# First MLP: gates and ups by seven block products for eight, plain downs woven between them, block sums from the attention's last head pair on

## The chip, the cores and the metric

The kernel runs on one core of one Trainium2 chip. Its five engines work from queues of their own and meet at semaphores: TensorE (PE in the profile; PEld is its weight load), VectorE (DVE), ScalarE (ACT), GpSimd (POOL) and SyncE (SP), which issues the loads. GpSimd issues a second kind of transfer, one that adds to what stands in memory. The metric is the device time of one execution in microseconds; less is better.

## The reference

A decoder trunk of two layers on 528 tokens (16 learned ones ahead of 512) with 1024 features: forgetting attention, a gated MLP, a gated linear recurrence (HGRN2), and a second gated MLP. All in float32. The part that the change touches is the MLP, here the first:

```python
def conv_ffn(h, norm_g, w_gate, w_up, conv_w, conv_b, w_down):
    xn = rms_norm(h, norm_g)
    a = xn @ w_gate                      # 1024 -> 2816
    ...
    a = (conv_b + conv_w[0] * a_pad[:, 0:L] + conv_w[1] * a_pad[:, 1:L + 1]
         + conv_w[2] * a_pad[:, 2:L + 2])    # causal, over the tokens
    return (jax.nn.silu(a) * (xn @ w_up)) @ w_down     # 2816 -> 1024
```

## The kernel before, in words

*Numbers.* Features lie on the partitions and tokens on the free axis. Every float32 operand of a matmul is split in two parts, hi and lo, and a product is three matmuls: hi by hi, hi by lo, lo by hi (`proj_unit`). `weights` loads one block of weights from HBM (SP, tile `raw`), copies it to `hi` (ScalarE, L210) and subtracts to get `lo` (VectorE, L126). The residual `h` stays in SBUF.

*Seven products for eight.* A product of 2 x 2 blocks is made from seven block products by Strassen's scheme in Winograd's form. It needs sums of weight blocks and sums of input blocks. The weights' sums are made ahead in HBM by DMA alone (`sum_blocks`): SP copies one block (L230) and GpSimd issues accumulating transfers on top (L232). For one key that is four copies and five accumulations, in four steps; accumulations onto the same sum, and the fourth sum, which takes in the second, wait for those before them. A generator, `summing`, holds all keys in order, and each call of `weights` (with `step` set) moves it one step on. The transfers go to SP's and GpSimd's queues, in order with what else stands there.

*Stages.* `fox` (attention) works on head pairs in a hand-written weave of generators; in its last turn, p = 7, `stage_p` makes early parts of the output projection, and after the turns the projection follows, with `summing` set ahead of it. `ffn0` is the first MLP, `hgrn` the recurrence, `ffn1` the second MLP.

*The first MLP (`ffn0`).* It has two runs of hidden features (`RUNS`: 2 x 6 and 2 x 5 blocks of 128). In each, `hidden` makes gate and up of one block with plain products (2 weights x 8 blocks x 3 matmuls x two halves of 264 tokens), the convolution, the gate; `forms` builds the seven input forms; then `down` multiplies by the down weights in seven block products for four pairs of output blocks. Sums are made of the down weights: 8 keys of 6 or 5 blocks' width. `hidden` has its memset of the first two columns of `A` on GpSimd (L1106).

*The second MLP (`ffn1`).* Its hidden pairs are split in five runs (`PAIRS`: 1, 2, 3, 2, 3 pairs of two blocks). The first pair (`plain`) uses plain products while the input forms are made. Every other pair uses `seven` twice, for its gates and its ups: seven products of 4 blocks x 3 matmuls, from the input forms and from a key's sums of gate or up weights. The downs (`down`) are plain products, woven between the next run's sevens:

```python
weave((chain(*steps), cost), side or (None, 1.0))
side = down(j0, hidden, i == len(runs) - 1), 5.3 * r
```

`weights` has four raw and four split buffers there (`self.more`), two and three elsewhere. Instructions are put in order per engine when the program is built, from the written order and a model of their times.

Of the kernel before, what the change touches and what calls it, by code (L numbers as in the profile page):

```python
# [12 lines left out]
F32 = mybir.dt.float32  # L13
# [8 lines left out]
P = 128  # L22
D = 1024
# [6 lines left out]
RUNS = [(0, 6), (12, 5)]  # L30
# [52 lines left out]
class Builder:  # L83
# [44 lines left out]
    def setup(self):  # L128
# [32 lines left out]
        self.summing = iter(())  # L161
        self.sqp = self.pool("sqp", 2)
# [19 lines left out]
    def weights(self, src, n, w=P, parts=1, step=True):  # L182
# [19 lines left out]
        if parts == 1:  # L202
            if isinstance(src, tuple):
                nc.sync.dma_start(raw[:, : n * w // 2], src[0])
                self.load = nc.sync.dma_start(raw[:, n * w // 2 :], src[1])
            else:
                self.load = nc.sync.dma_start(raw, src)
            if step:
                next(self.summing, None)
            nc.scalar.copy(hi, raw)  # L210
            self.sub(lo, raw, hi.bitcast(F32))
            return u
# [3 lines left out]
    def sum_blocks(self, key, blocks, joined=False):  # L216
# [7 lines left out]
        sums = [new(i, n) for i in range(2 if joined else 4)]  # L224
        if joined:
            both = new(2, 2 * n)
            sums += [both[:, :n], both[:, n:], both]
        s1, s2, s3, s4 = sums[:4]
        for out, x, *rest in (s1, w21, w22), (s2, w21, w22, w11), (s3, w11, w21), (s4, w12, s2):
# [3 lines left out]
            if out is s4:  # L233
                self.sums[key] = sums
            yield 1

    def down_blocks(self, mp, c0, r):

        w = self.a["dn0"]
        return [w[2 * mp + m][:, (c0 + k * r) * P : (c0 + k * r + r) * P] for m in range(2) for k in range(2)]  # L240

    def hidden_blocks(self, j, i):

        w = self.a["gu1"]
        return [w[2 * j + m, i][:, 4 * k * P : 4 * k * P + 4 * P] for m in range(2) for k in range(2)]

    def all_sums(self):
        for c0, r in RUNS:
            for mp in range(KT // 2):
                yield from self.sum_blocks((0, mp, c0), self.down_blocks(mp, c0, r))  # L250
        for j in range(PAIRS[0], NF // 2):
            for i in range(2):
                yield from self.sum_blocks((1, j, i), self.hidden_blocks(j, i), True)
# [127 lines left out]
    def fox(self, ctx):  # L381
# [285 lines left out]
        for p in range(-3, NPAIR):  # L667
            fill, cost = [], 0.0
# [33 lines left out]
        self.summing = self.all_sums()  # L702
# [117 lines left out]
    def hgrn(self, ctx):  # L820
# [237 lines left out]

        plan = {5: (0, 1, 2), 6: (3, 4, 5), 7: (6, 7)}
# [21 lines left out]
    def ffn0(self, ctx):  # L1081
        nc, a = self.nc, self.a
        layer, a0, o0 = 0, 0, 0
        ga, up = (halves(t0) if T - t0 > 512 else [(t0, T - t0)] for t0 in (a0, o0))
        gcol, cw, cb = ((V_FFN0, V_CW0, V_CB0), (V_FFN1, V_CW1, V_CB1))[layer]
        sp = self.pool(f"ffn1_{layer}", 1, ctx=ctx)
        s2 = self.pool(f"ffn2_{layer}", 2, ctx=ctx)
        self.normsplit(gcol, a0)
        segs = (SEG0, SEG1)[layer]
        am, rs = self.token_stats(segs)  # L1090
        self.spread_rs(rs, segs)
        def unit(w, toks, x):
            for t0, tn in toks:
                ps = self.anybank()[:, :tn]
                for _ in self.proj_unit(ps, w, x, t0, tn):
                    pass
                yield ps, t0, tn

        n = T - o0
        hw = n // 2  # L1100

        def hidden(m, early=None):

            A, t, s = (temp(w, nm) for w, nm in ((T + 2, "A"), (n, "t"), (n, "s")))
            if o0 == 0:
                nc.gpsimd.memset(A[:, 0:2], 0.0)  # L1106
            wg, wu = (self.weights(a[f"gu{layer}"][m, i], KT) for i in range(2))
            if early is not None:
                early()
            for ps, t0, tn in unit([wg], ga, self.x):  # L1110
                nc.vector.tensor_tensor(A[:, 2 + t0 : 2 + t0 + tn], ps, self.rsb[:, t0 : t0 + tn], ALU.mult)
            c0 = cw + 3 * m
            nc.scalar.activation(
                t, A[:, o0 + 2 : T + 2], AF.Identity, scale=self.vcol(c0 + 2), bias=self.vcol(cb + m)
            )
            nc.vector.scalar_tensor_tensor(t, A[:, o0 + 1 : T + 1], self.vcol(c0 + 1), t, ALU.mult, ALU.add)
            nc.vector.scalar_tensor_tensor(t, A[:, o0:T], self.vcol(c0), t, ALU.mult, ALU.add)
            self.act(s, t, AF.Silu)
            nc.vector.tensor_tensor(t, s, self.rsb[:, o0:], ALU.mult)
            for ps, t0, tn in unit([wu], up, self.x):  # L1120
                tv = t[:, t0 - o0 : t0 - o0 + tn]
                nc.vector.tensor_tensor(tv, ps, tv, ALU.mult)
            return t

        def temp(w, name):
            return s2.tile([P, 6 * P], F32, name=name, tag="temp", bufs=8)[:, :w]

        def put_form(f, j, x, fhi, flo):
            x = x.rearrange("p (f t) -> p f t", t=hw)
            f = slice(f, f + x.shape[1])  # L1130
            nc.scalar.copy(fhi[:, f, j, :], x)
            self.sub(flo[:, f, j, :], x, fhi[:, f, j, :].bitcast(F32))

        def forms(j, c0, r, fhi, flo, early):

            form = lambda f, x: put_form(f, j, x, fhi, flo)
            t1 = hidden(c0 + j)
            x11, x12 = t1[:, :hw], t1[:, hw:]
            ta, tb = temp(n, "ta"), temp(n, "tb")
            self.sub(ta[:, :hw], x11, x12)  # L1140
            form(0, x11)
            form(3, ta[:, :hw])
            t2 = hidden(c0 + r + j, early)
            x21, x22 = t2[:, :hw], t2[:, hw:]
            nc.vector.scalar_tensor_tensor(ta[:, hw:], ta[:, :hw], -1.0, x22, ALU.mult, ALU.subtract)
            form(4, ta[:, hw:])
            form(1, t2)
            self.sub(tb[:, :hw], x22, x12)
            nc.vector.scalar_tensor_tensor(tb[:, hw:], ta[:, hw:], -1.0, x21, ALU.mult, ALU.subtract)
            form(5, tb)  # L1150

        def parts(raw):

            w = raw.shape[1]
            hi = self.whi.tile([P, 8 * P], F32R, name="hi", tag="hi")[:, :w]
            lo = self.wlo.tile([P, 8 * P], F32R, name="lo", tag="lo")[:, :w]
            nc.scalar.copy(hi, raw)  # L1157
            self.sub(lo, raw, hi.bitcast(F32))
            return hi, lo

        def left(mp, c0, r, i):


            raw = temp(r * P, "left")
            if isinstance(i, int):
                src = self.sums[layer, mp, c0][i - 1]
            else:
                k0 = (c0 + i[1] * r) * P
                src = a[f"dn{layer}"][2 * mp + i[0]][:, k0 : k0 + r * P]
            nc.sync.dma_start(raw, src)  # L1170
            return parts(raw)

        def down(mp, c0, r, fhi, flo, last, first):

            def product(ps, w, f, start):
                hi, lo = w
                mm = nc.tensor.matmul  # L1180
                for k in range(r):
                    c = slice(k * P, k * P + P)
                    xh, xl = fhi[:, f, k, :], flo[:, f, k, :]
                    mm(ps, hi[:, c], xh, start=start and k == 0, stop=False, skip_group_check=not start)  # L1184
                    mm(ps, hi[:, c], xl, start=False, stop=False, skip_group_check=not start)  # L1185
                    mm(ps, lo[:, c], xh, start=False, stop=k == r - 1, skip_group_check=not start)  # L1186

            def put(m, half, ps, op, store=False):
                c = o0 + half * hw
                hv = self.h[:, 2 * mp + m, c : c + hw]  # L1190
                nc.vector.tensor_tensor(hv, hv, ps, op)
                if store and last and layer == 1:
                    nc.sync.dma_start(a["out"][2 * mp + m][:, half * hw : half * hw + hw], hv)

            A, D = (self.bank("p")[:, :hw] for _ in range(2))
            B, C = (self.bank(x)[:, :hw] for x in "cd")
            ws = lambda i: left(mp, c0, r, i)
            product(A, first[0] if first else ws((0, 0)), 0, True)
            nc.scalar.copy(B, A)
            product(D, first[1] if first else ws(1), 3, True)  # L1200
            put(1, 1, D, ALU.subtract)
            product(B, ws(2), 4, False)
            nc.scalar.copy(C, B)
            put(0, 1, B, ALU.add)
# [8 lines left out]
            if last and layer == 0:  # L1213
                self.sumsq(2 * mp)
                self.sumsq(2 * mp + 1)
# [317 lines left out]
```

## Time and profile before

| what | value |
|---|---|
| time, median of 3 runs (lowest to highest) | 1459.96 us (1459.2 to 1460.03) |
| the profiled execution's own time | 1463.9 us |
| its span | 1462.0 us |
| TensorE, share of the span | 98% |
| VectorE, ScalarE, GpSimd | 67%, 45%, 10% |
| mean granted TensorE clock | 0.994 |
| moved by DMA | 230.97 MB, mean 158 GB/s |
| first MLP, first to last matmul | 390.9 to 763.6 us |
| recurrence | about 764 to 1103 us |
| second MLP | about 1103 to 1462 us |

Durations and windows below are in microseconds from the span's start. The DMA share of a window is the mean busy share of the core's 16 DMA engines; q1 is the queue of SP's transfers, q0 that of GpSimd's. A matmul's record is longer than the distance to the next, since matmuls overlap, so the pace is read from counts or from starts.

### The profile page before, as it was taken

The numbers are of one execution on the slowest core, as the hardware profiler recorded it, in microseconds if no ns is written. First come the engines' busy times: TensorE is split into PE (matmuls) and PEld (weight loads), VectorE is DVE, ScalarE is ACT, GpSimd is POOL, SyncE is SP. The second block draws the span as 40 slices with busy tenths as digits, with TensorE's granted clock in tenths as the row PEclk, the third lists the DMA queues.
The fourth block names the chain that finished last, engine by engine and source line by source line (L and its number), as shares of the span: only waits on it lengthen the run. The fifth ranks groups of instructions, "written<-read, shape, count | busy, mean of one in ns | idle before, by whom it ended". The sixth has DMA issues, their size and how long they took to land.

```text
span 1462.0 us, 29172 instructions
## 1 busy us (share of the span) xinstructions
PE 1435.2 (98%) x11482; PEld 1349.0 (92%) x11482; DVE 974.9 (67%) x2079; ACT 663.1 (45%) x1293; POOL 150.2 (10%) x265
## 2 busy tenths in 40 slices
PE   7999999999999999999999999999999999999998
PEld 6888888888999999999999999999999889999997
DVE  6555555774667675666785667587567777866773
ACT  5355555563434444333563224333345565544551
POOL 6000000001112100112001101011111110000000
PEclk9999999999999999999999999999999999999999
DMA  4433334435999884678737617374587795544542
GB/s 160 119 105 90 90 90 123 124 99 137 293 231 247 213 254 137 171 193 197 218 92 181 168 22 181 91 178 103 126 238 169 208 265 162 173 143 137 161 146 85
DMA packets 99696, 230.97 MB, mean 158 GB/s; under 512 B 13528, under 2 KB 15320, under 8 KB 99560
## 3 DMA queue, kind: packets, MB, share of 16 engines
q1 hardware_dynamic: 79400, 188.47, 40.3%
q0 software_dynamic: 20160, 40.64, 18.3%
q8 instruction: 90, 1.47, 0.4%
q14 instruction: 46, 0.38, 0.1%
HBM read 213.62 MB, written 75.24 MB: 198 GB/s over the span
## 4 chain that ended last, share of the span: by engine, by line
PE 91%; DMA 4%; DVE 2%; ACT 1%; issue 1%; SPq 1%; ACTq 0%; DVEq 0%
PE psp L263 9%; PE psp L267 9%; PE psp L266 9%; PE pss L263 8%; PE pss L267 8%; PE pss L266 8%; PE psp L312 5%; PE psc L797 2%; PE psp L1292 2%; PE psp L1290 2%; PE psp L1291 2%; PE psp L1184 1%; PE psp L1186 1%; PE psp L1185 1%; PE pss L951 1%; PE psd L1292 1%
## 5 line engine op out<-in xcount | busy, mean ns | idle before, releaser
L210 ACT CAST hi<-raw 128x1024 fp32r<-128x1024 f32 (+3 forms) x250 | 234.1, 939 | 381.3 <-PE psp L266 96.1
L126 DVE TENSOR_TENSOR lo<-raw,hi 128x1024 fp32r<-128x1024 f32 (+3 forms) x254 | 275.5, 1088 | 100.9 <-ACT hi L210 96.8
L263 PE MATMUL psp<-xhi,hi 128*128 128x264 f32 (+1 forms) x984 | 283.9, 290 | 6.1 <-ACT xhi L332 6.1
L266 PE MATMUL psp<-xlo,hi 128*128 128x264 f32 (+1 forms) x984 | 283.6, 288 | 3.2 <-DVE xlo L333 3.2
L267 PE MATMUL psp<-xhi,lo 128*128 128x264 f32 (+1 forms) x984 | 283.9, 289 | 0.0
L263 PEld LDWEIGHTS psp<-xhi,hi 128*128 128x128 f32 x984 | 186.8, 190 | 10.7 <-ACT xhi L332 6.1
L266 PEld LDWEIGHTS psp<-xlo,hi 128*128 128x128 f32 x984 | 187.1, 190 | 6.0 <-DVE xlo L333 3.7
L267 PEld LDWEIGHTS psp<-xhi,lo 128*128 128x128 f32 x984 | 187.0, 190 | 1.7 <-issue 1.6
L267 PE MATMUL pss<-xhi,lo 128*128 128x264 f32 (+3 forms) x520 | 149.8, 288 | 0.0
L263 PE MATMUL pss<-xhi,hi 128*128 128x264 f32 (+3 forms) x520 | 149.1, 287 | 0.0
L266 PE MATMUL pss<-xlo,hi 128*128 128x264 f32 (+3 forms) x520 | 149.1, 287 | 0.0
L232 POOL DMA_DIRECT2D s<-gu x80 | 66.4, 856 | 332.3 <-DMA s<-gu 300.9
L263 PEld LDWEIGHTS pss<-xhi,hi 128*128 128x128 f32 x520 | 97.8, 188 | 0.6
L267 PEld LDWEIGHTS pss<-xhi,lo 128*128 128x128 f32 x520 | 97.7, 188 | 0.7
L266 PEld LDWEIGHTS pss<-xlo,hi 128*128 128x128 f32 x520 | 97.7, 188 | 0.7
L263 PE MATMUL pss<-room,hi 128*128 128x512 f32 (+1 forms) x182 | 69.6, 387 | 1.7 <-ACT hi L210 1.7
L267 PE MATMUL pss<-room,lo 128*128 128x512 f32 (+1 forms) x182 | 70.4, 387 | 0.0
L266 PE MATMUL pss<-room,hi 128*128 128x512 f32 (+1 forms) x182 | 70.2, 386 | 0.0
L312 PE MATMUL psp<-hi,xhi 128*128 128x256 f32 x232 | 66.9, 288 | 2.5 <-ACT v L599 2.5
L1292 PE MATMUL psp<-xhi,lo 128*128 128x258 f32 x240 | 67.9, 283 | 0.9 <-DVE lo L126 0.8
L1157 ACT CAST hi<-left 128x768 fp32r<-128x768 f32 (+1 forms) x56 | 43.4, 781 | 54.0 <-PE psp L1185 18.3
L1290 PE MATMUL psp<-xhi,hi 128*128 128x258 f32 x240 | 67.6, 282 | 0.0
(488 smaller groups left out, 3798.1 us busy)
## 6 DMA issues: line engine op xcount, KB each, us to landing
raw<-gu SPq DMA_DIRECT2D x48, 512.0 KB
s<-gu SPq DMA_DIRECT2D x80, 256.0 KB
s<-gu POOLq DMA_DIRECT2D x80, 256.0 KB, 6.0
raw<-gu SPq DMA_DIRECT2D x60, 256.0 KB
pk<-stg SPq DMA_DIRECT2D x48, 264.0 KB
raw<-s SPq DMA_DIRECT2D x40, 256.0 KB
raw<-s SPq DMA_DIRECT2D x20, 512.0 KB
raw<-wqk SPq DMA_DIRECT2D x14, 512.0 KB
```

What stands on the lines that cost most here:

```text
L126: self.nc.vector.tensor_tensor(out, x, y, ALU.subtract)
L210: nc.scalar.copy(hi, raw)
L232: nc.gpsimd.dma_start(out, y, accum_op=ALU.add, max_dma_last_dim=4 * n)
L263: ins = mm(ps, hi[:, i, :], xh, start=k == 0, stop=False)
L266: mm(ps, hi[:, i, :], xl, start=False, stop=False)
L267: mm(ps, lo[:, i, :], xh, start=False, stop=k == total - 1)
L312: mm(ps[:tn, :256], y[:, t0 : t0 + tn], w, start=n == 0, stop=n == 23)
L797: ins = mm(o, v[:kn, j, 2 * (p % 2) + hd, :], w[hd][0], start=j == 0, stop=j == last)
L1157: nc.scalar.copy(hi, raw)
L1290: mm(ps, hi[:, k0 + k, :], xh, start=start and k == 0, stop=False, skip_group_check=not start)
L1291: mm(ps, hi[:, k0 + k, :], xl, start=False, stop=False, skip_group_check=not start)
L1292: mm(ps, lo[:, k0 + k, :], xh, start=False, stop=k == 3, skip_group_check=not start)
```

## The change

`ffn0` and its helpers go, and `ffn1` becomes `ffn(ctx, layer, a0, o0)`, called for both MLPs. For the first one that means: gates and ups of pairs 1 to 10 by `seven` (on halves of 264 tokens), pair 0 plain, all downs plain (two halves of 264) and woven with the next run, buffers as in the second. The sums are now of both layers' gate and up weights, 20 keys each, in order of layer; none of down weights. `summing` starts ahead of the attention's last turn. A call of `weights` moves it `rate` steps on: 1 in the attention, 2 during an MLP's plain pair, 1 in its other runs, 2 in the recurrence. A `seven` has two stepping loads instead of one. The first MLP's `A` tiles keep the memset on GpSimd, one for each pair.

```diff
-            if step:
+            for _ in range(self.rate if step else 0):
                 next(self.summing, None)
...
-        sums = [new(i, n) for i in range(2 if joined else 4)]
-        if joined:
-            both = new(2, 2 * n)
-            sums += [both[:, :n], both[:, n:], both]
-        s1, s2, s3, s4 = sums[:4]
+        s1, s2, s34 = new(1, n), new(2, n), new(3, 2 * n)
+        s3, s4 = s34[:, :n], s34[:, n:]
...
     def all_sums(self):
-        for c0, r in RUNS:
-            for mp in range(KT // 2):
-                yield from self.sum_blocks((0, mp, c0), self.down_blocks(mp, c0, r))
-        for j in range(PAIRS[0], NF // 2):
-            for i in range(2):
-                yield from self.sum_blocks((1, j, i), self.hidden_blocks(j, i), True)
+        for layer in range(2):
+            for j in range(PAIRS[0], NF // 2):
+                for i in range(2):
+                    yield from self.sum_blocks((layer, j, i), self.hidden_blocks(layer, j, i))
...
         for p in range(-3, NPAIR):
+            if p == NPAIR - 1:
+                self.summing = self.all_sums()
...
-        self.summing = self.all_sums()
         for m in range(KT):
...
+        self.rate = 2
         plan = {5: (0, 1, 2), 6: (3, 4, 5), 7: (6, 7)}
...
-    def ffn0(self, ctx):
...
-    def ffn1(self, ctx):
+    def ffn(self, ctx, layer, a0, o0):
...
-            u = self.weights(s34, KT, step=False)
+            u = self.weights(s34, KT)
...
         def new_pair(nm):
-            return s2.tile([P, 2, T + 2], F32, name=nm, tag=nm)
+            t = s2.tile([P, 2, T + 2], F32, name=nm, tag=nm)
+            if nm == "A" and o0 == 0:
+                nc.gpsimd.memset(t[:, :, 0:2], 0.0)
+            return t
...
-                for t0, tn in ((0, n // 2), (n // 2, n // 2)) if last and m == KT - 1 else ((0, n),):
+                for t0, tn in [(o0, n // 2), (o0 + n // 2, n // 2)] if last and m == KT - 1 else out_runs:
...
+                if last and layer == 0:
+                    self.sumsq(m)
...
         for i, (j0, r, hidden) in enumerate(runs):
             steps = []
+            self.rate = 1 if i else 2
...
-            b.ffn0(c1)
+            b.ffn(c1, 0, 0, 0)
...
-            b.ffn1(c1)
+            b.ffn(c1, 1, A1, NM)
```

More of the change, by code (lines that the diff above doesn't have):

```diff
@@ L29 @@
 NEARLY = 4
-RUNS = [(0, 6), (12, 5)]
 PAIRS = [1, 2, 3, 2, 3]
@@ L161, in setup @@
         self.summing = iter(())
+        self.rate = 1
         self.sqp = self.pool("sqp", 2)
@@ L214, in weights, with sum_blocks @@
         return *u, [partial(load, slice(i * m, i * m + m)) for i in range(parts)]
-    def sum_blocks(self, key, blocks, joined=False):
+    def sum_blocks(self, key, blocks):
         nc = self.nc
@@ L233, in sum_blocks, with hidden_blocks @@
             if out is s4:
-                self.sums[key] = sums
+                self.sums[key] = s1, s2, s34
             yield 1
[L237 to L244, printed above, removed]
+    def hidden_blocks(self, layer, j, i):
+        w = self.a[f"gu{layer}"]
         return [w[2 * j + m, i][:, 4 * k * P : 4 * k * P + 4 * P] for m in range(2) for k in range(2)]
     def all_sums(self):
-        for c0, r in RUNS:
-            for mp in range(KT // 2):
-                yield from self.sum_blocks((0, mp, c0), self.down_blocks(mp, c0, r))
-        for j in range(PAIRS[0], NF // 2):
-            for i in range(2):
-                yield from self.sum_blocks((1, j, i), self.hidden_blocks(j, i), True)
+        for layer in range(2):
+            for j in range(PAIRS[0], NF // 2):
+                for i in range(2):
+                    yield from self.sum_blocks((layer, j, i), self.hidden_blocks(layer, j, i))
     def proj_unit(self, ps, units, x, t0, tn, prev=None):
@@ L1078, in hgrn @@
             self.sumsq(m, A1)
-    def ffn0(self, ctx):
+    def ffn(self, ctx, layer, a0, o0):
         nc, a = self.nc, self.a
-        layer, a0, o0 = 0, 0, 0
-        ga, up = (halves(t0) if T - t0 > 512 else [(t0, T - t0)] for t0 in (a0, o0))
+        mm = nc.tensor.matmul
+        g0 = a0 // 4 * 4
+        gw = (T - g0) // 2
+        n = T - o0
+        ga, up, out_runs = (halves(t0) if T - t0 > 512 else [(t0, T - t0)] for t0 in (a0, o0, o0))
         gcol, cw, cb = ((V_FFN0, V_CW0, V_CB0), (V_FFN1, V_CW1, V_CB1))[layer]
@@ L1087, in ffn0 @@
         s2 = self.pool(f"ffn2_{layer}", 2, ctx=ctx)
-        self.normsplit(gcol, a0)
+        self.more = [self.pool(f"{nm}{layer}", b, ctx=ctx) for nm, b in (("wraw_", 2), ("whi_", 1), ("wlo_", 1))]
+        self.nweights = -1
+        self.normsplit(gcol, g0)
         segs = (SEG0, SEG1)[layer]
@@ L1091, in ffn0 @@
         self.spread_rs(rs, segs)
[L1092 to L1204, printed above, removed]
-            product(A, ws((0, 1)), 1, False)
-            put(0, 0, A, ALU.add, True)
-            product(C, ws(3), 5, False)
-            put(1, 1, C, ALU.subtract, True)
-            product(D, ws(4), 2, False)
-            put(0, 1, D, ALU.add, True)
-            product(C, ws((1, 1)), 6, False)
-            put(1, 0, C, ALU.subtract, True)
-            if last and layer == 0:
-                self.sumsq(2 * mp)
-                self.sumsq(2 * mp + 1)
@@ L1218, in ffn0 @@
-        for x in "cd":
-            nc.tensor.matmul(self.bank(x)[:, :hw], self.xhi[:, 0, :P], self.xhi[:, 0, :hw], start=True, stop=True)
-        for c0, r in RUNS:
-            fhi, flo = (sp.tile([P, 7, 6, hw], F32R, name=nm, tag=nm)[:, :, :r, :] for nm in ("fhi", "flo"))
-            first = []
-            for j in range(r):
-                early = None if j < r - 1 else lambda: first.append([left(0, c0, r, i) for i in ((0, 0), 1)])
-                forms(j, c0, r, fhi, flo, early)
-            for mp in range(KT // 2):
-                down(mp, c0, r, fhi, flo, c0 > 0, first.pop() if first else None)
@@ L1230, in ffn1 @@
-    def ffn1(self, ctx):
-        nc, a = self.nc, self.a
-        mm = nc.tensor.matmul
-        o0 = NM
-        g0 = A1 // 4 * 4
-        gw = (T - g0) // 2
-        n = T - o0
-        gcol, cw, cb = V_FFN1, V_CW1, V_CB1
-        sp = self.pool("ffn1_1", 1, ctx=ctx)
-        s2 = self.pool("ffn2_1", 2, ctx=ctx)
-        self.more = [self.pool(nm, b, ctx=ctx) for nm, b in (("wraw1", 2), ("whi1", 1), ("wlo1", 1))]
-        self.nweights = -1
-        self.normsplit(gcol, g0)
-        am, rs = self.token_stats(SEG1)
-        self.spread_rs(rs, SEG1)
@@ L1280, in seven @@
             B, C = (self.bank(x)[:, :gw] for x in "cd")
-            w11, w12, _, w22 = self.hidden_blocks(j, i)
-            while (1, j, i) not in self.sums:
+            w11, w12, _, w22 = self.hidden_blocks(layer, j, i)
+            while (layer, j, i) not in self.sums:
                 next(self.summing)
-            s1, s2_, _, _, s34 = self.sums[1, j, i]
+            s1, s2_, s34 = self.sums[layer, j, i]
             def product(ps, unit, k0, f, start):
@@ L1343, in plain @@
             for m in range(2):
-                wg = self.weights(a["gu1"][2 * j + m, 0], KT)
-                for t0, tn in halves(A1):
+                wg = self.weights(a[f"gu{layer}"][2 * j + m, 0], KT)
+                for t0, tn in ga:
                     ps = self.bank("s")[:, :tn]
@@ L1350, in plain @@
                 input_forms(2 * m)
-                wu = self.weights(a["gu1"][2 * j + m, 1], KT)
-                ps = self.bank("s")
-                yield from self.proj_unit(ps, [wu], self.x, o0, n)
-                nc.vector.tensor_tensor(t[:, m, :], ps, t[:, m, :], ALU.mult)
+                wu = self.weights(a[f"gu{layer}"][2 * j + m, 1], KT)
+                for t0, tn in up:
+                    ps = self.bank("s")[:, :tn]
+                    yield from self.proj_unit(ps, [wu], self.x, t0, tn)
+                    tv = t[:, m, t0 - o0 : t0 - o0 + tn]
+                    nc.vector.tensor_tensor(tv, ps, tv, ALU.mult)
                 input_forms(2 * m + 1)
@@ L1400, in down @@
             for m in range(KT):
-                w = self.weights(a["dn1"][m][:, c0 : c0 + k * P], k)
-                for t0, tn in ((0, n // 2), (n // 2, n // 2)) if last and m == KT - 1 else ((0, n),):
+                w = self.weights(a[f"dn{layer}"][m][:, c0 : c0 + k * P], k)
+                for t0, tn in [(o0, n // 2), (o0 + n // 2, n // 2)] if last and m == KT - 1 else out_runs:
                     ps = self.bank("s")[:, :tn]
-                    yield from self.proj_unit(ps, [w], hidden, t0, tn)
-                    hv = self.h[:, m, o0 + t0 : o0 + t0 + tn]
+                    yield from self.proj_unit(ps, [w], hidden, t0 - o0, tn)
+                    hv = self.h[:, m, t0 : t0 + tn]
                     nc.vector.tensor_tensor(hv, hv, ps, ALU.add)
-                    if last:
-                        nc.sync.dma_start(a["out"][m][:, t0 : t0 + tn], hv)
+                    if last and layer == 1:
+                        nc.sync.dma_start(a["out"][m][:, t0 - o0 : t0 - o0 + tn], hv)
+                if last and layer == 0:
+                    self.sumsq(m)
         for x in "cd":
@@ L1433, in ffn1 @@
         weave(side)
+        self.more = None
 def trace(tc, a, stop=None):
```

## Prediction

> **What bounds the kernel now.** I read the page's engine line and slices first, then the stages by windows, then the first MLP's edges in the instruction timeline. The page: spans, busy times, TensorE and DMA by slices, DMA queues.
>
> ```profile
> span 1462.0 us, 29172 instructions
> PE 1435.2 (98%) x11482; PEld 1349.0 (92%) x11482; DVE 974.9 (67%) x2079; ACT 663.1 (45%) x1293; POOL 150.2 (10%) x265
> ...
> PE   7999999999999999999999999999999999999998
> ...
> DMA  4433334435999884678737617374587795544542
> ...
> q1 hardware_dynamic: 79400, 188.47, 40.3%
> q0 software_dynamic: 20160, 40.64, 18.3%
> ```
>
> TensorE is busy nearly everywhere, so fewer matmuls should be less time; but the DMA row already stands at 9 where the first MLP begins (slice 10). The windows below (engine busy, count; granted clock, DMA share, GB/s) are the first MLP, its gate/up part, the recurrent layer, and two stretches of the second MLP.
>
> ```profile
> 391.00:767.00 376.00, 375.58 (x3090) 374.90 (x3092) 260.99 (x441) 160.62 (x234) 50.84 (x95) 1.00 0.76 198
> 500.00:600.00 100.00, 100.00 (x823) 100.00 (x822) 63.72 (x98) 40.05 (x57) 6.97 (x12) 1.00 0.64 184
> 768.00:1103.00 335.00, 334.86 (x3125) 320.50 (x3124) 224.53 (x591) 116.31 (x216) 44.70 (x68) 1.00 0.58 144
> 1134.00:1197.00 63.00, 58.73 (x428) 54.81 (x427) 49.04 (x76) 34.41 (x62) 10.61 (x13) 1.00 0.87 236
> 1196.00:1278.00 82.00, 82.00 (x598) 77.92 (x597) 64.99 (x98) 48.34 (x83) 1.63 (x2) 1.00 0.60 182
> ```
>
> The first MLP loses nothing: 375.58 of 376 us. One matmul of 264 columns costs 100/823 = 0.1215 us. The second MLP has the structure that the first is to get. Where block sums are still being made (1134 to 1197) it idles 63 - 58.73 = 4.3 us at a DMA share of 0.87; where hardly any are (1196 to 1278) it idles nothing at 0.60. VectorE at 49.0/63 and 65.0/82 us, 78 and 79%, does not bind. So two things decide: the matmuls saved, and whether the DMA engines carry weights and sums together.
>
> **The change, part by part.**
>
> *Matmuls.* First and last of the stage:
>
> ```profile
> 390.89 0.29 PE L263 MATMUL pss<-xhi,hi 128*128 128x264 f32 x1
> 763.61 0.28 PE L1186 MATMUL psd<-fhi,lo 128*128 128x264 f32 x1
> ```
>
> Before: gates and ups 22 x 2 weights x 8 x 3 x 2 halves = 2112, downs 4 x 21 x (6 + 5) = 924; together 3036, by 0.1215 = 368.9 us of the 372.7 between the rows. After: the plain pair 192, twenty sevens (one pair's gates or ups) of 7 x 4 x 3 = 84, 1680, plain downs 8 x 22 x 3 x 2 = 1056; 2928. Saved 108 x 0.1215 = **13.1 us**, all on the path.
>
> *Input forms, copies, adds* move to ScalarE and VectorE as in the second MLP; by its 79% with no idle TensorE, nothing. If that cover went, the plain stretch would pay first, by a microsecond.
>
> *DMA in the first MLP.* What a megabyte costs, as time of all 16 engines, from the queues' shares in 408 to 500 (first two rows) and in 1136 to 1200 (last two):
>
> ```profile
> q0 software_dynamic: 3056, 7.35, 49.9%
> q1 hardware_dynamic: 4587, 13.69, 42.6%
> ...
> q1 hardware_dynamic: 6465, 12.04, 57.2%
> q0 software_dynamic: 1851, 3.38, 32.0%
> ```
>
> Loads and copies (q1): 92 x 0.426/13.69 = 2.86, and 64 x 0.572/12.04 = 3.04; I take 2.95 us per MB. Accumulations (q0, issued by GpSimd): 6.25 and 6.06; I take 6.15. One key (a pair's gates or ups) now needs four copies and five accumulations of 0.262 MB: 1.05 x 2.95 + 1.31 x 6.15 = 11.2 us of DMA. A seven loads 1.835 MB, a down 65.5 KB for each of its k blocks. A step (a quarter key) goes with two loads of each seven and each down's load. The runs, TensorE against DMA:
> - run 1: 5 sevens x 10.2 + 96 down matmuls = 62.7 us. 10.22 MB loads, 18 steps: 4.72 MB copies, 5.90 MB accumulations: 80.4 us. Overdraft 17.7.
> - run 2: 6 sevens, 192: 84.6 us. 13.1, 5.24, 6.55 MB: 94.4. Overdraft 9.8.
> - run 3: 4 sevens, 288: 75.8 us. 10.5, 4.19, 5.24 MB: 75.5. None.
> - run 4: 5 sevens, 192: 74.4 us. 11.3, 4.72, 5.90 MB: 83.5. Overdraft 9.1.
>
> Together **36.6 us**. That an overdraft is paid is seen in the second MLP's run 1. Rows: three 512-wide/258-wide borders for the pace, and ScalarE's copy that comes once per seven.
>
> ```profile
> 1299.84 0.40 PE L266 MATMUL pss<-room,hi 128*128 128x512 f32 x1
> ...
> 1302.39 0.28 PE L1290 MATMUL psc<-xfhi,hi 128*128 128x258 f32 x1
> ...
> 1303.82 0.40 PE L263 MATMUL pss<-room,hi 128*128 128x512 f32 x1
> ...
> 1144.38 0.36 ACT L1297 COPY psc<-psp 128x258 f32<-128x258 f32 x1 [1.11 <-PE psp L1292]
> ...
> 1196.82 0.37 ACT L1297 COPY psc<-psp 128x258 f32<-128x258 f32 x1
> ...
> 1278.46 0.36 ACT L1297 COPY psc<-psp 128x258 f32<-128x258 f32 x1
> ```
>
> Eleven wide matmuls take 2.55 us (0.232 each), twelve of 258 take 1.43 (0.119). A seven with its 1.6 downs should take 84 x 0.119 + 9.6 x 0.232 = 12.2 us. Its DMA (2.6 steps) is 2.73 MB x 2.95 + 0.85 x 6.15 = 13.3. Measured: (1196.82 - 1144.38)/4 = 13.1. The DMA sets the pace, at its full share. In run 2 six take 81.6 us, as their matmuls do. The waits on the chain there show it as loads that land late:
>
> ```profile
> 1149.04 8.05 DMA raw<-s
> ...
> 1161.09 8.57 DMA raw<-gu
> ...
> 1176.01 7.64 DMA raw<-dn
> ```
>
> How much of the 36.6 us shows? Between 0 (all of it deferred) and 36.6. What can be deferred: in the plain stretch (192 x 0.1215 = 23.3 us) about two keys' accumulations are still under way, 16 us, so that some 6 us are left to load run 1 ahead; SP runs up to eight weights ahead (four raw, four split buffers), some 18 us, and from there about 11 us more pass to a pair's convolution, which lets GpSimd lag 29 us, 1.5 keys, 12 us of accumulations; and the 11 steps after the memset of pair 10 are needed by nobody in this stage, of their accumulations 7.6 us count. 36.6 - 6 - 12 - 7.6 = **11 us lost**. The nearest row, run 1 of the second MLP, paid 4.3 us of an overdraft of 5 x 1.1, more than three quarters; but there SP fed GpSimd no faster than it accumulated, so nothing could lag. Here a key is due every 14 to 19 us and can. That rate of payment is the rival below.
>
> *New waits.* SP waits for a sum before it loads it; behind that wait stand the downs' loads and the copies of later keys, and TensorE starves about 18 us on. GpSimd's queue now holds twenty keys' accumulations, and between them the memset of A's two first columns for each pair (the gates' convolution on VectorE waits for it, and behind that the splits of all weights). GpSimd's pace:
>
> ```profile
> s<-gu POOLq DMA_DIRECT2D x80, 256.0 KB, 6.0
> ...
> 961.45 1.97 POOL L232 DMA_DIRECT2D s<-gu  x2
> 970.19 1.84 POOL L232 DMA_DIRECT2D s<-gu  x2 [6.77 <-DMA s<-gu]
> 980.10 0.81 POOL L232 DMA_DIRECT2D s<-s  x1 [7.95 <-DMA s<-gu]
> ...
> DVE t L1116 <- POOL A L1106: 6.7, 2, 5.2
> POOL st L923 <- PE pss L1021: 38.9, 4, 17.1
> ```
>
> A key is two landings in sequence: 12 us by the median, 18.7 from 961.45 to 980.10. The runs ask a key every 14 to 19 us. So GpSimd just follows; VectorE has waited for this memset before (6.7 us).
>
> The Trainium skill, "DMA: Bandwidth & Descriptors", section "Anatomy of one DMA", gives about 2.0 us plus bytes over 436 GB/s for such a transfer, an estimate of 2.6 us here; the landing of 6.0 us above contradicts it, and the measurement decides. By that page two landings would be 5.2 us and GpSimd would never lag.
>
> The attention before that, by windows:
>
> ```profile
> 40.00:340.00 300.00, 291.99 (x2274) 252.41 (x2273) 177.49 (x544) 160.90 (x465) 4.11 (x29) 0.99 0.39 104
> ```
>
> *Sums from the attention's last pair on* (four steps, beside small loads) and the plain pair's double rate: nothing, for the DMA share is 0.39 in the attention; at worst 2 us where four 256 KB copies stand ahead of the row loads.
>
> *The recurrent layer at rate 2.* 60 steps instead of 40: 5 keys x 11.2 = 56 us more DMA in a window of 335 at share 0.58, which leaves 141. GpSimd's memsets now queue behind twice the accumulations; it had 17.1 us of waiting to give in the row above. At the start two or three keys' lag may meet the memsets of this layer. I take **+2 us** with the term before, between 0 and 10.
>
> *The second MLP* finds its sums made: run 1 then has 10.2 MB x 2.95 = 30 us of DMA in 61, and the 4.3 us go: **-4**, between -4.3 and 0.
>
> Sum: -13.1 + 11 - 4 + 2 = -4.1 us. The profiled execution took 1463.9 us, 1.9 around its span, and 3.9 over the timed median of 1459.96; the sum would give a span of 1458 and a timed 1455.9 us.
>
> **The rivals.**
> - *The sums fit.* All of the overdraft is deferred, or the engines take more than I price. For it: the gate/up part before carries nearly that much without loss (a load with its step, 0.917 MB x 2.95 + 0.49 x 6.15 = 5.7 us of DMA in 48 x 0.1215 = 5.8). Against: run 1 of the second MLP. Then -13.1 - 4 = -17: **1443 us**. The Trainium skill, same page, section "Specifications", gives a ceiling of 435 GB/s; by it run 1's 20.8 MB would be an estimate of 48 us in 62.7, which is this rival; no window quoted here exceeds 236 GB/s.
> - *The other side: GpSimd's queue couples everything.* Since each pair's memset of A stands in order behind the accumulations issued so far, no sum can lag, VectorE stops at the convolution, and the splits behind it stop TensorE. The overdraft shows up to pair 10's memset: 36.6 - 6 - 3 = 28 us. It gives -13.1 + 28 - 4 + 2 = +13: **1473 us**. It decides once more than 15 us of the 36.6 come through, that is, if a key takes GpSimd above some 18 us. For it: the 18.7 us above, and the three quarters paid in the second MLP, which would be 28 of 36.6 too. Against: 12 by the median landing.
>
> **How the numbers follow.** Partly paid overdraft 0.44, own range 1449 to 1464; sums fit 0.22; GpSimd couples 0.34. The runs before spread 0.06%; 0.2%, 2.9 us, is about what a measurement tells from no change. Of the first case 0.26 is faster, 0.13 within, 0.05 slower: faster 0.22 + 0.26 = 0.48, same 0.13, slower 0.34 + 0.05 = 0.39. The range 1441 to 1476 takes in both rivals and leaves out heavier losses at the recurrent layer's start.
>
> **What would show it.** TensorE count lower by 108; idle TensorE in the first MLP near 11 us, most in the first 65 us of sevens with the pace near 14 to 15 us a seven; DMA share 0.9 or more through it; loads of raw landing after 8 us on the chain; the second MLP's 1134 to 1197 stretch without idle time and no accumulations there. Wrong if TensorE idles under 5 us in the first MLP, if VectorE's waits for GpSimd's memset exceed 10 us, or if the recurrent layer grows by more than 8.

## The result, and the profile after

The change makes the kernel slower: 1474.74 us median (1466.68 to 1479.78) against 1459.99 (1456.56 to 1465.2) for the kernel before in the same comparison, a ratio of 1.0092 with a 95% interval of 1.0064 to 1.0119. The forecast was 1455.9; the measured time lies inside its range, on the other side of no change. The profiled execution took 1475.14 us with a span of 1473.4, against 1463.9 and 1462.0 before.

The page of the kernel after: span, busy times, slices of TensorE and of the DMA engines, and the landing of GpSimd's accumulations (number, KB each, median us).

```profile
span 1473.4 us, 29291 instructions
PE 1433.4 (97%) x11374; PEld 1343.8 (91%) x11374; DVE 987.0 (67%) x2094; ACT 699.2 (47%) x1380; POOL 197.8 (13%) x314
...
PE   7999999999998899999999999999999999999999
...
DMA  4433335465989999999999977598142455544442
...
s<-gu POOLq DMA_DIRECT2D x160, 256.0 KB, 7.4
```

The matmuls saved are there: 11482 - 11374 = 108. So is the cost: from slice 10 to 22 the DMA row stands at 8 or 9, and TensorE falls to 8 in two slices where it had 9 before.

Where the time went is read from edges. First the kernel before, then after: the first matmul of the first MLP (for before it stands in the prediction, 390.89), and the statistics matmuls with which the recurrence and the second MLP open.

```profile
769.38 0.50 PE L355 MATMUL psc<-onesd,ss 128*128 128x2 f32 x4
...
1112.04 0.50 PE L355 MATMUL psd<-onesd,ss 128*128 128x2 f32 x4
```

```profile
390.11 0.29 PE L253 MATMUL pss<-xhi,hi 128*128 128x264 f32 x1
...
786.14 0.50 PE L345 MATMUL psc<-onesd,ss 128*128 128x2 f32 x4
...
1129.74 0.50 PE L345 MATMUL psd<-onesd,ss 128*128 128x2 f32 x4
```

First MLP with the first steps after it: 378.5 before, 396.0 after, **+17.5 us**. Attention, up to that first matmul: -0.8. Recurrence: 342.7 and 343.6, +0.9. Second MLP: 350.0 and 343.7, -6.3. The whole loss is in the first MLP, where 13.1 us of matmuls were saved: some 30 us of TensorE were lost there.

By windows of the first MLP, before and then after (busy time and count of TensorE, its weight loads, VectorE, ScalarE, GpSimd; granted clock, DMA share, GB/s):

```profile
391.00:440.00 49.00, 49.00 (x407) 49.00 (x406) 32.78 (x66) 18.31 (x25) 8.66 (x14) 1.00 0.97 243
440.00:570.00 130.00, 130.00 (x1071) 130.00 (x1070) 89.25 (x147) 53.24 (x77) 18.08 (x29) 1.00 0.86 228
570.00:700.00 130.00, 130.00 (x1071) 130.00 (x1070) 87.07 (x139) 50.20 (x70) 19.84 (x32) 1.00 0.69 174
```

```profile
391.00:440.00 49.00, 45.77 (x330) 43.70 (x328) 35.97 (x67) 26.50 (x39) 11.88 (x18) 0.90 0.95 243
440.00:570.00 130.00, 117.31 (x920) 114.05 (x919) 93.14 (x150) 68.19 (x119) 29.85 (x41) 0.99 1.00 270
570.00:700.00 130.00, 127.29 (x1031) 126.86 (x1030) 87.95 (x140) 61.42 (x100) 29.08 (x38) 0.99 1.00 265
700.00:781.00 81.00, 81.00 (x666) 81.00 (x665) 54.84 (x92) 38.60 (x61) 21.42 (x26) 1.00 1.01 268
...
1152.00:1215.00 63.00, 62.58 (x473) 59.91 (x472) 53.72 (x83) 39.02 (x69) 0.00 (x0) 1.00 0.51 160
```

Counts tell more than busy time, since a matmul's record is longer than its pace. A full window holds one matmul per 0.1215 us: 403, 1070, 1070, 667. Missing are 73, 150, 39 and 1, or **8.9 + 18.2 + 4.7 + 0.1 = 31.9 us**. The DMA share is 1.00 from 440 to the stage's end: no slack anywhere, where before it had been 0.86 and 0.69. The last row answers to 1134 to 1197 of before: the second MLP's first run has no accumulations left and no idle time to speak of.

The chain shows the waits as loads of weights (raw from gu, from dn, or from the sums s), on which TensorE's chain stands for 6 to 11 us at a time:

```profile
452.78 7.13 DMA raw<-gu
...
472.53 7.11 DMA raw<-s
...
496.81 8.32 DMA raw<-s
517.62 10.92 DMA raw<-s
...
555.35 8.40 DMA raw<-gu
```

No making of a sum stands between them, and among SP's own waits from 391 to 790 none holds a load back for a sum. The loads are slow with every DMA engine busy.

### The profile page after: what moved, and what is told of

It is laid out like the page before. It is cut to its first block, busy times and chain, and to the rows that moved or that the text cites. A ratio compares the mean times of both kernels' runs of the same rounds, so it can differ in the third digit from the quotient of the medians.

```text
span 1473.4 us, 29291 instructions
## 1 busy us (share of the span) xinstructions
PE 1433.4 (97%) x11374; PEld 1343.8 (91%) x11374; DVE 987.0 (67%) x2094; ACT 699.2 (47%) x1380; POOL 197.8 (13%) x314
## 4 chain that ended last, share of the span: by engine, by line
PE 80%; DMA 10%; DVE 6%; ACT 2%; issue 2%; SPq 1%; ACTq 0%; DVEq 0%
PE psp L253 7%; PE pss L253 7%; PE pss L257 7%; PE pss L256 6%; PE psp L256 6%; PE psp L257 6%; PE psp L302 5%; DMA raw<-gu 4%; PE psp L1134 4%; PE psp L1136 4%; PE psp L1135 4%; DVE lo L125 2%; PE psc L788 2%; PE psd L1134 2%; PE psd L1136 2%; PE psd L1135 2%
## 5 line engine op out<-in xcount | busy, mean ns | idle before, releaser
L125 DVE TENSOR_TENSOR lo<-raw,hi 128x1024 fp32r<-128x1024 f32 (+2 forms) x334 | 342.0, 1029 | 160.8 <-ACT hi L210 156.2
L253 PE MATMUL psp<-xhi,hi 128*128 128x264 f32 (+2 forms) x752 | 217.5, 291 | 6.5 <-ACT xhi L322 6.5
L256 PE MATMUL psp<-xlo,hi 128*128 128x264 f32 (+2 forms) x752 | 218.3, 291 | 2.6 <-DVE xlo L323 2.6
L257 PE MATMUL psp<-xhi,lo 128*128 128x264 f32 (+2 forms) x752 | 217.8, 290 | 0.0
L253 PE MATMUL pss<-room,hi 128*128 128x264 f32 (+2 forms) x534 | 169.5, 320 | 2.1 <-ACT hi L210 2.1
L256 PE MATMUL pss<-room,hi 128*128 128x264 f32 (+2 forms) x534 | 170.2, 319 | 0.0
L257 PE MATMUL pss<-room,lo 128*128 128x264 f32 (+2 forms) x534 | 169.8, 320 | 0.1
L1134 PE MATMUL psp<-xhi,hi 128*128 128x264 f32 (+1 forms) x480 | 136.9, 285 | 5.0 <-ACT A L1217 4.2
L1136 PE MATMUL psp<-xhi,lo 128*128 128x264 f32 (+1 forms) x480 | 136.9, 285 | 2.0 <-DVE lo L125 2.0
L1135 PE MATMUL psp<-xlo,hi 128*128 128x264 f32 (+1 forms) x480 | 136.2, 284 | 0.0
L253 PEld LDWEIGHTS pss<-room,hi 128*128 128x128 f32 x534 | 100.6, 189 | 6.8 <-ACT hi L210 2.5
L256 PEld LDWEIGHTS pss<-room,hi 128*128 128x128 f32 x534 | 100.5, 188 | 4.8
```

Of the source, the lines that this page charges most:

```text
L125: self.nc.vector.tensor_tensor(out, x, y, ALU.subtract)
L253: ins = mm(ps, hi[:, i, :], xh, start=k == 0, stop=False)
L256: mm(ps, hi[:, i, :], xl, start=False, stop=False)
L257: mm(ps, lo[:, i, :], xh, start=False, stop=k == total - 1)
L1134: mm(ps, hi[:, k0 + k, :], xh, start=start and k == 0, stop=False, skip_group_check=not start)
L1135: mm(ps, hi[:, k0 + k, :], xl, start=False, stop=False, skip_group_check=not start)
```

## The experiments

Three theories. D: the 16 DMA engines are full in the first MLP, and every copy and accumulation beyond what fits is paid in time. G: it is GpSimd's in-order queue, by the memset of A or by sums that are late. The first two runs below can't tell D from G, since with the accumulations gone GpSimd's queue is empty too; the waits above and the third run bear on G. S: it is the structure itself: buffers, VectorE, the start.

**No sums' traffic.** In `sum_blocks`, keys of the first MLP make nothing and hand the sevens other blocks of the same size:

```
+ if key[0] == 0:
+     for step in range(4):
+         if step == 3:
+             self.sums[key] = w21, w22, self.a["gu0"][2 * key[1] + 1, key[2]]
+         yield 1
+     return
```

> Leaves out all making of the first MLP's 20 keys of sums (copies and accumulations): its sevens load other weight blocks of the same size instead, so the numbers of that layer are not the reference's. Theory D (the 16 DMA engines are full, every copy and accumulation is paid in time): the DMA share of the first MLP falls from 1.00 to about 0.5 and some 20 us of its waits go; left are the start's 9 us; about 1453 us. Theory G (GpSimd's in-order queue holds up the memset of A): the same, since that queue is empty too. Theory S (the structure: split buffers, VectorE's 70 to 90% in the first runs, the start): the waits stay, 1468 us or more.

Measured 1454.98 us (before 1460.5; ratio 0.9963, 0.9949 to 0.9978). Its windows:

```profile
400.00:410.00 10.00, 7.38 (x41) 6.29 (x41) 8.32 (x19) 2.54 (x5) 0.00 (x0) 0.82 0.30 100
410.00:420.00 10.00, 10.00 (x72) 10.00 (x71) 4.56 (x9) 3.29 (x6) 0.00 (x0) 0.84 0.01 2
...
440.00:570.00 130.00, 130.00 (x1068) 129.70 (x1067) 106.63 (x173) 76.18 (x129) 0.51 (x5) 1.00 0.50 162
```

Without the traffic the loss after 440 is gone: 1068 matmuls instead of 920. The loss at the start is not: 41 and 72 matmuls where 10 us hold 82, with the DMA engines mostly idle. So there are two losses, and only the one after 440 can belong to D.

**Copies without accumulations**, left out for the first MLP's keys alone:

```
- for y in rest:
+ for y in rest if key[0] else ():
```

> Leaves out the accumulations of the first MLP's sums alone; its copies stay, so the sums are not sums. D: accumulations are 5.9 of 20.8 MB in run 1 but 36 of its 80 us of DMA; with them gone every run fits (44, 54, 43, 47 us of DMA in 63, 85, 76, 74): nearly all of the loss of e1 is gained back, about 1455 us. If copies (memory to memory) were the costly part: half of e1's gain at most, 1464 us. S: 1468 or more.

Measured 1455.87 us (ratio 0.9975, 0.9958 to 0.9993), with 1037 matmuls in 440 to 570 at a DMA share of 0.71. Of the 19.8 us between the changed kernel and the one without the traffic, 18.9 come back with the accumulations alone left out, by the medians. In the changed kernel, from 440 to 570, they are 26% of the bytes, but 43% of the engines' time:

```profile
q1 hardware_dynamic: 13333, 25.84, 56.8%
q0 software_dynamic: 4972, 9.06, 43.1%
```

That is 130 x 0.431/9.06 = 6.18 us per MB against 130 x 0.568/25.84 = 2.86 for copies and loads.

**The memset on VectorE.**

```
- nc.gpsimd.memset(t[:, :, 0:2], 0.0)
+ nc.vector.memset(t[:, :, 0:2], 0.0)
```

> The memset of A's first two columns on VectorE in place of GpSimd; all sums as they are. D: no change, 1475 within 4 us. G: VectorE and with it the splits no longer wait for GpSimd's queue, the waits go, about 1455 us.

Measured 1480.0 us (ratio 1.0136, 1.0095 to 1.0178): no gain. The waits of the changed kernel agree (engine, tile and line, what released it: us in total, times, longest). From 391 to 790 GpSimd waits for its own accumulations, and the memset of A waits 1.5 us in all; no row has VectorE waiting for it.

```profile
POOL s L229 <- DMA s<-gu: 270.7, 56, 10.6
...
POOL A L1184 <- DVE t L1166: 1.5, 1, 1.5
```

**Sums from head pair 4 on**, to spread the traffic into the attention.

```
- if p == NPAIR - 1:
+ if p == NPAIR - 4:
```

> The sums start ahead of the attention's turn p = 4 in place of p = 7; each load there moves them one step, some 13 to 16 steps more (3 to 4 keys, 36 to 45 us of DMA) ahead of the first MLP, where the DMA share was 0.39. D: run 1 and run 2 lose less, the waits of the first MLP shrink by 10 to 15 us, 1460 to 1465 us, if the attention's small row transfers don't pay for it. G: the same or less. S: no change, 1475.

Measured 1477.73 us (ratio 1.0124, 1.0097 to 1.015): a miss for D as I had put it. An earlier start moves which keys are made, not how many steps go with the first MLP's loads, and those were left as they were. By edges the first MLP took 0.8 us less than in the changed kernel, and the attention 5.7 more. Its window still reads full:

```profile
440.00:570.00 130.00, 121.22 (x947) 118.63 (x946) 96.74 (x154) 71.25 (x124) 26.83 (x37) 0.97 0.99 268
```

**Input forms behind the scale row.** At the start VectorE's written order mixes input forms and splits with the small steps of the norm's scale row. These are lines of the changed kernel; `rsb` is the row, and the scaling of the gates, L1195, waits for it:

```profile
404.10 0.42 DVE L1108 SCALAR_TENSOR_TENSOR room<-room 128x264 f32<-128x264 f32 x1
...
404.51 1.25 DVE L125 TENSOR_TENSOR xflo<-room,xfhi 128x1056 fp32r<-128x1056 f32 x1
...
406.82 0.16 DVE L335 TENSOR_TENSOR run<-rqn 128x6 f32<-128x6 f32 x1
...
412.59 0.42 DVE L368 COPY rsb<-psc 128x256 f32<-128x256 f32 x1
...
413.61 0.77 DVE L1195 TENSOR_TENSOR A<-pss,rsb 128x264 f32<-128x264 f32 x2
```

Until 413.6 no result of a gate is read out of its bank (the memory that TensorE writes to), and TensorE's plain matmuls stop at 402.9 and come back at 418.2. Of what it does between, the trace names 3.1 us of waits, all for VectorE: 2.1 for `xflo` (the split input forms), 0.7 for `lo`, 0.3 for a step of the scale row.

```profile
400.00:410.00 10.00, 7.15 (x49) 6.15 (x48) 9.70 (x16) 6.41 (x8) 3.40 (x6) 0.92 1.06 244
410.00:420.00 10.00, 9.73 (x45) 8.88 (x45) 6.42 (x15) 3.80 (x8) 2.46 (x3) 0.56 1.09 296
```

In the second window PE is "busy" 9.73 us with 45 matmuls, because the granted clock fell to 0.56 after the stall: from 414.7 to 418.5 matmuls start 0.22 us apart instead of 0.12. The Trainium skill, "TensorE: Matmul & The Clock Gate", section "What's actually happening", says that TensorE gets half its clock after an idle window of about 3.4 us. The half agrees with the 0.22 us here; an idle stretch of that length does not show, since the longest wait here is 1.4 us. The edit orders the forms behind the row:

```
- nc.vector.tensor_copy(self.rsb[:, b0:e0], ps[:, : e0 - b0])
+ self.rsb_last = nc.vector.tensor_copy(self.rsb[:, b0:e0], ps[:, : e0 - b0])
...
+ if layer == 0:
+     self.after(ins, self.rsb_last)      # ins: the forms' first subtraction
```

> The first MLP's input forms are ordered on VectorE behind the row scales (rsb); all else as in the change. The start's stall (TensorE 49 and 45 matmuls in 400 to 410 and 410 to 420, where 84 fit) should go: if it is VectorE's order, 5 to 9 us, 1466 to 1470 us. If it is the late weights (7.8 us landing in a full DMA), the stall stays, 1475.

Measured 1474.95 us (ratio 1.0111, 1.008 to 1.0142), as long as the changed kernel. Its windows say why:

```profile
400.00:410.00 10.00, 8.12 (x54) 7.90 (x53) 9.30 (x21) 4.49 (x6) 3.36 (x8) 0.83 1.05 268
410.00:420.00 10.00, 10.00 (x84) 10.00 (x83) 9.41 (x12) 3.65 (x6) 3.29 (x6) 1.00 0.82 178
391.00:440.00 49.00, 46.06 (x364) 45.43 (x362) 38.36 (x71) 26.24 (x41) 13.44 (x20) 0.97 0.95 249
440.00:570.00 130.00, 118.11 (x901) 115.74 (x902) 92.59 (x148) 68.79 (x120) 28.41 (x39) 0.95 0.99 264
```

The second 10 us are full, the first are not yet. 34 matmuls are won before 440 and 19 lost from there to 570. My reading: while TensorE stalls, the DMA engines go on moving; take the stall away and TensorE comes sooner to the same full engines.

**The start and the traffic both taken away**: the first edit and the last together.

> Leaves out the sum making for the first MLP's blocks (its sevens load other blocks of the same size) and puts the input forms behind the scale row on VectorE: both losses that the runs so far have named are gone, so what is left is the structure itself. S (the start is VectorE's order, some 6 us of matmuls missing in 400 to 420 without sums: 41 and 72 of 84 in each): about 4 to 6 us below the run without sums alone, 1449 to 1451 us, with 52 or more matmuls in 400 to 410 and all 84 in 410 to 420. If the start were another cause: 1455 again. With D and S both gone the matmul term (108 x 0.1215 = 13.1 us) should be nearly the whole difference to the kernel before: 1447 to 1450; if a third loss is in the structure, over 1453.

Measured 1449.87 us (before 1459.48; ratio 0.9917, 0.9885 to 0.995), 85 and 84 matmuls in the two 10 us windows. The forms' order is worth some 5 us (1454.98 to 1449.87) where the engines have room and nothing where they don't. With both causes gone, the change gains 9.6 us by the medians, over all stages. By the same edges as above, in the profiled executions, the first MLP takes 364.9 us, 13.6 less than before: the whole matmul term, so no third loss is left in it. The second MLP takes 343.9, and the recurrence 348.0, 5.4 more than before. From 105 to 165 us after its opening TensorE makes 555 matmuls, 592 in the kernel before, and it waits 3.2 us for a tile of VectorE's (`qp`). The changed kernel makes 594 there, with the DMA engines as busy (0.92 in the first 30 us of both), so full engines alone don't explain it; the cause was not looked for.

**Sums from head pair 0, one step for each seven, no double rate.** This spreads the same keys over attention and MLP.

```
- if p == NPAIR - 1:
+ if p == 0:
...
- u = self.weights(s34, KT)
+ u = self.weights(s34, KT, step=False)
...
- self.rate = 1 if i else 2
+ self.rate = 1
```

> The sums start at the attention's turn p = 0 and go slower: one step for a seven in place of two, rate 1 in the plain pairs. Some 8 keys come ahead of the first MLP, and 64 steps in it in place of 88 and more. D: run 1 wants 66.5 us of DMA in 62.7, runs 2 to 4 fit (78 in 85, 65 in 76, 70 in 74): about 4 us of loss there, the start's 9 stay, and the attention pays some 4 to 10 us (e4: 4 for three turns): 1456 to 1464 us. G (late sums): SP waits for sums and it stays above 1470.

Measured 1473.51 us (ratio 1.0099, 1.0082 to 1.0115), a miss. The MLP does recover (rows two and three), by edges 12.8 us of the 17.5, but the attention now pays 11.9: 367 matmuls in its last 51 us, 403 in the changed kernel, and the first MLP's scale row comes some 10 us later (422.0 instead of 411.8).

```profile
340.00:391.00 51.00, 47.44 (x367) 43.73 (x368) 28.17 (x62) 22.09 (x47) 6.50 (x8) 0.97 0.58 139
...
440.00:570.00 130.00, 121.43 (x966) 119.26 (x965) 98.71 (x157) 72.66 (x126) 20.08 (x29) 0.99 0.87 233
570.00:700.00 130.00, 130.00 (x1070) 130.00 (x1069) 91.67 (x145) 63.97 (x104) 22.28 (x30) 1.00 0.91 243
```

At a share of 0.58 the attention still loses. I take it that its small transfers queue behind 256 KB copies; that was not tried by itself.

**Three plain pairs.** The other way to relieve the engines: pairs 0 to 2 by plain products, sevens from pair 3 on (16 keys instead of 20), one step for each seven and no double rate in the first pair.

```
+ FIRST = [3, 1]
...
- for j in range(PAIRS[0], NF // 2):
+ for j in range(FIRST[layer], NF // 2):
...
- if i == 0:
+ if j < FIRST[layer]:
      steps.append(plain(j, hidden))
...
- if j == PAIRS[0]:
+ if j == FIRST[layer]:
```

> In the first MLP pairs 0 to 2 are plain (run 0 and run 1), sevens from pair 3; 16 keys in place of 20; one step for a seven, rate 1 in plain pairs; sums from p = 7 as in the change. 48 matmuls more, 5.8 us. D: the DMA fits in every run (60 in 58, 78 in 85, 65 in 76, 70 in 74), left are the start's stall and the second MLP's 6 us gained: -13.1 + 5.8 + 9 - 6 = -4, 1456 us. S: above 1470.

Measured 1461.67 us (ratio 1.0009, 0.9995 to 1.0023): the DMA loss is gone (1067 matmuls in 440 to 570 at a share of 0.88), and 48 matmuls of the saving with it; the start is worse, with 20 and 54 matmuls in 400 to 410 and 410 to 420, and the time is above the 1456 that D gave. With the forms behind the scale row besides:

> c1 with e5's order. D with the start explained by VectorE's order: 1448 to 1451 us, below the kernel before by 9 to 12. If the start is late weights: as c1, 1456.

Measured **1455.01 us** (before 1459.24; ratio 0.9974, 0.996 to 0.9989), some microseconds above what I expected, and faster than both kernels. Two things stand in its trace that the expectation left out: the recurrence takes 348.7 us instead of 342.7, and 400 to 410 still holds only 43 matmuls.

```profile
400.00:410.00 10.00, 7.06 (x43) 6.52 (x43) 9.38 (x22) 4.69 (x6) 4.22 (x6) 0.83 1.01 229
...
440.00:570.00 130.00, 128.99 (x1059) 128.57 (x1058) 95.88 (x151) 68.19 (x112) 21.98 (x33) 1.00 0.90 236
```

**Two plain pairs** (`FIRST = [2, 1]`), else the same.

> Two plain pairs instead of three ahead of the sevens, one step for each seven, input forms behind the scale row. 24 matmuls fewer than with three plain pairs (2.9 us), two keys more of 11.2 us of DMA. D: the DMA share stood at 0.88 to 0.90 in the first MLP with three plain pairs; two keys are 22 us of DMA in some 370, so about 0.95: with room, 1452 to 1454; if the first runs are overdrawn again, 1455 to 1459 and below 1060 matmuls in 440 to 570.

Measured 1470.22 us (ratio 1.0073, 1.0049 to 1.0098): 15 us for two more keys, far beyond the engines' price of them, with 937 matmuls in 570 to 700 at a share of 0.95. The chain goes through another thing here, the making of a sum:

```profile
583.38 4.25 DMA s<-gu
...
588.14 6.13 DMA s<-gu
...
594.56 0.80 POOL s L230
...
600.47 6.29 DMA s<-s
606.78 4.15 DMA raw<-s
```

Accumulations in sequence, GpSimd between them, then the load that waited. From 570 to 700 SP waits 41.9 us in all for sums before it can load them. With fewer steps per seven the sums seem to have lost their lead. To test that, the double rate in the first pair was given back, four steps or one key of lead:

> Two plain pairs as in the run that came out at 1470 us, but with the double rate in the first pair, so that four steps (one key) more are made there. In that run the chain passes through the making of a sum (583 to 607 us: two accumulations of a quarter key in sequence, GpSimd, a third, then the load of the sum). L (late sums: no lead over GpSimd's serial landings): one key of lead more takes most of that wait away, 1453 to 1460 us, with over 1020 matmuls in 570 to 700 (937 there). D (the engines are full, the sum was late only because of that): the same traffic a little earlier, 1465 to 1472.

Measured 1463.93 us (ratio 1.0025, 1.0008 to 1.0041). 6.3 of the 15 us come back, with 998 matmuls in 570 to 700: between the two expectations. So the lead is part of it. What is left has the same form at 662 to 683 us (accumulations of 4.2, 7.1 and 5.5 us in sequence on the chain, and a load of s), at a DMA share of 0.81 there, so not with full engines; whether still more lead would remove it was not tried. Late sums, part of theory G, exist, then, but in these kernels with one step a seven, not in the changed kernel, where neither the chain nor SP's waits hold any of them.

## Why the prediction was wrong

- *Matmuls*: right, 108 fewer.
- *Unit prices*: right, 2.86 and 6.18 us per MB against 2.95 and 6.15 taken.
- *Overdraft of 36.6 us*: of the right size; 31.9 us are lost, start included, and with the start repaired, taking the sums' traffic away brings 25.1 us (1474.95 to 1449.87).
- *Deferral*: **the step that failed**, "36.6 - 6 - 12 - 7.6 = 11 us lost". 22.9 us are missing from 440 to 700 alone. Work put off is only saved if it lands where the engines have slack or leaves the stage. The rows of the changed kernel from 440 to 781 (the queues, and the copies and accumulations that were issued) show neither:

```profile
q1 hardware_dynamic: 32342, 65.43, 54.6%
q0 software_dynamic: 13929, 25.37, 45.3%
...
s<-gu POOLq DMA_DIRECT2D x78, 256.0 KB, 7.4
s<-gu SPq DMA_DIRECT2D x77, 256.0 KB
...
s<-s POOLq DMA_DIRECT2D x19, 256.0 KB, 5.6
```

  Accumulations of 25.37 MB, where the four runs were priced at 23.6: nothing has left the stage. Copies and loads are 65.4 MB, priced at 64.0. The engines' time is 341 us of 341. The 12 us of lag do not show: GpSimd issued 97 accumulations to SP's 77 copies, five to four as a key asks, and up to 440 it was level too (33 to 27). Counted up to 440, 503, 570, 640, 700 and 781 it is never more than four accumulations behind. The prediction set the second MLP's run 1 aside because "SP fed GpSimd no faster than it accumulated, so nothing could lag"; the same held here. A lag would have had nowhere to go in any case: run 3 was priced at 75.5 us of DMA in 75.8. The 6 us of loading ahead in the plain stretch were not there either: the window 391 to 440 already stood at 0.95. Only the 7.6 us may have held, for from 700 on TensorE lost 0.1 us; without the other two terms the sum would have been 29.
- *The nearest row, rightly seen and set aside*: run 1 of the second MLP had paid more than three quarters of its overdraft. By that rate 28 of 36.6 would show. With the start repaired, 39 + 169 + 32 matmuls are missing in the three windows to 700, the last 32 being 1070 - 1038 in 570 to 700: 240 x 0.1215 = 29 us. The rival used this number, and its 1473 us came out; its mechanism did not, so its time was luck. VectorE never waited for the memset, and moving it gained nothing.
- *The start*: not in the sum at all. "TensorE, nothing" for the input forms named the plain stretch as the first to pay, "by a microsecond"; 8.9 us are missing there, of which some 5 show as soon as the engines have room. The busy share of VectorE that the prediction went by is of later windows of the second MLP, and a share does not show that the scale row stands in the queue behind the forms.
- *Second MLP*: -6.3, forecast -4 with a bound of -4.3, so slightly more than the idle time of the one window. Where the rest comes from was not looked into. *Recurrence and attention*: +0.9 and -0.8, forecast +2 together. That +0.9 is one profile: in those of the other runs the recurrence took from 1.3 to 8.5 us more than before.
- *Signs to look for*: pace of a seven in the first run 14 to 15 us: from ScalarE's copies below, (497.59 - 437.94)/4 = 14.9. DMA share over 0.9: right, and loads of raw that take over 8 us on the chain. The second MLP's first run without accumulations: right. Idle near 11 us: wrong.

```profile
437.94 0.37 ACT L1141 COPY psc<-psp 128x264 f32<-128x264 f32 x1
...
497.59 0.37 ACT L1141 COPY psc<-psp 128x264 f32<-128x264 f32 x1
```

In sum: -13.1 + 31.9 - 6.3 + 0.9 - 0.8 = +12.6 against a span longer by 11.4; counting missing matmuls at full pace is no finer than that.

What stays open: why one plain pair more or less moves the late sums so much (1455.0, 1463.9 or 1470.2 us), why the recurrence takes up to 8.5 us more in the other runs, and whether a finer spacing of steps would let the attention carry keys without loss.

## What to carry to other kernels

Where a saving in matmuls is bought with transfers, add up the engines' time over the whole stage, accumulations at their own price, and set it against the stage's new, shorter time: here that excess is about what was lost. Do not subtract a queue's lag before its counts show that it lags and that there is slack behind it. When a nearby stage shows the rate at which an overdraft is paid, take that rate before an argument for why it should be lower here. And fixing one stall in a stage that is bound elsewhere shows nothing by itself: try it together with the other bound removed.

## What the runs showed of the hardware

A megabyte accumulated in HBM by DMA cost the 16 engines 2.2 times a megabyte loaded or copied (6.18 and 2.86 us, in 440 to 570 of the changed kernel), and with full engines the median accumulation of 256 KB took 7.4 us to land, where it was 6.0 over the kernel before. With every engine busy they moved 265 to 270 GB/s of this mix. A stall of a few microseconds cost TensorE more than itself: in the 10 us after it the granted clock was 0.56, which is 4.4 us at full speed.
